# Compressed scores per block, uf written as x2 comes, token scale ahead of later splits, last stores on two queues

## The chip, the cores and the metric

The kernel runs on one core of one Trainium2 chip. The metric is the device time of one execution in microseconds; lower is better. The core's engines run their own instruction streams in order and wait for one another by semaphores: PE (TensorE) multiplies, DVE (VectorE) and ACT (ScalarE) work on elements, POOL (GpSimd) adds a few tiles, SP (SyncE) starts transfers.

## The reference

Two blocks follow one another on 256 tokens of width 2048. The first has one layer: attention with a compressed, a selected and a windowed branch (16 heads of 64, 4 key groups), a gating unit, a merge, and an added gate. The second puts 16 meta tokens in front (272 tokens) and has two layers, the first with a bidirectional state-space scan and a convolution of 31 taps, the second with neighbourhood attention. What the change touches:

```python
def first_block(x, p, ...):
    h = rms_norm(x, norm_g)                       # token scale
    q, kv, g_logits, z_a, uv, z_b, merge_logits = jnp.split(h @ w_in, SPLIT_IDX, axis=-1)
    ...
    kc = compress(k_c, pe_k, w1_k, w2_k)          # 15 blocks of keys
    sc = jnp.einsum('bqgrd,bngd->bgrqn', qb, kc) * scale   # compressed scores
    ...
    x = x + merged @ w_out
    x = x + jax.nn.sigmoid(x @ w_ple_gate) * (p @ w_ple)   # x2 in the kernel
    return rms_norm(x, final_g)

def second_block(x, meta_tokens, ...):
    h = jnp.concatenate([meta, x], axis=1)
    h = even_layer(h, ...)      # u = rmsnorm(h, norm_g); proj = u @ w_in; SSD scan, conv, w_out
    h = odd_layer(h, ...)       # neighbourhood attention
    return rmsnorm(h, final_norm_g)[:, N_META:]
```

## The kernel before

All activations lie with their features on the 128 partitions, 16 chunks of 128 features by 256 or 272 tokens. Most projections are "split": weights and activations are each written as a high and a low part (wh and wl, xh and xl, uh and ul), and `mm3` issues three matmuls for a chunk (L120 to L122). A weight piece of 512 KB is fetched by SP into one of four raw buffers; ACT writes its high half (L98), DVE its low half (L99). The first NFIRST = 2 projections of block 1 and the projections NAT = 0 to 3 of layer e take f32 operands and one f32 matmul for a chunk (L156); each shows as two records in the trace.

The order of the instructions on each engine is set by the scheduler of the framework from the order of the code and from priorities: `K.later(n)` puts a piece n places later in priority, `issue_after(ins)` keeps a piece behind an instruction. Each engine then runs its list strictly in order. Pools give out memory; a tile that takes the place of an earlier one waits for the earlier one's last reader.

**Start.** Squares of x are summed per token (`tok_sum`), the reciprocal root is made by `rsqrt` and `newton` on tiny tiles (rs_v, rs_y, ...), `r` is copied (L303), spread over the partitions by `diag` and the matmul `rb` (L218, L219), and copied by ACT to `rbs` (L305). Every projection of block 1 is multiplied by `rbs` as it leaves PSUM (`pj`, L319).

**Compressed scores.** The compressed keys are split into kcbd; the eight query projections are split into qh and ql; behind the last one a loop of 2 x 8 `mm3` of 32 columns makes `scps`, and DVE adds the bias (`sc`, L447).

**Boundary.** In the last stage of block 1, for each of 16 chunks, `w_pg`'s projection passes through ACT (`zt`), two DVE operations to x2 (L659, L660), its weighted square `sqw` (L663), and a plain square on ACT (`sq`). POOL adds the squares, weighted ones to s2 and plain ones to s1. Then PE makes the sum ss12 of s2 and the last sqw (L672, L673), and the token sums ss1 of s1 (L210, three matmuls of two records). Layer e reads ss12: `v` (L698), ten Newton steps on 272 columns, the scale r12 (a tile named tmp). `uf` is x2 times the two gains: the meta columns on DVE (L703), the chunks c % 4 == 1 on DVE (L707), the others on ACT (L709). `un` is uf times r12 (L714), split into uh (ACT, L163) and ul (DVE, L164). The projections 0 and 1 use uf, then `e_w_dt` uses uh and ul with 64 output rows (dt), then projections 2 and 3 use uf, then all others uh and ul. ss1 gives a second scale rbh, with which `norm_out` (L724) rewrites x2 as the residual and stores it to hres in four transfers.

**Later stages.** dt passes through a short chain (`steps`), its running sums go out to memory and come back, `dtp` transposes them; `cacc` is the short convolution, `cbps`, `xtp`, `yps` belong to the scan, with masks `m` from DVE.

**End.** The final scale is spread in `frb`, DVE multiplies h in five pieces (L1236), and SP stores each (L1237).

## Time and profile before

| | |
|---|---|
| time, median of 3 runs (lowest to highest) | 2270.6 us (2270.43 to 2271.83) |
| the profiled execution | 2271.78 us, its span 2269.9 us |
| PE busy | 2218.4 us, 98% of the span |
| DVE busy | 1639.2 us, 72% |
| ACT busy | 1162.1 us, 51% |
| POOL busy | 121.3 us, 5% |
| HBM read | 391.45 MB, 174 GB/s over the span |

The times in the views count from the span's start. Busy time of an engine says little by itself; what matters is what an engine waits for, and whether the engine that waits is the one on which the end depends. PEclk is the clock that PE was granted, as a share of full speed: 1.00 is 2.4 GHz, 0.50 is 1.2 GHz.

### The profile page before, as it was taken

How to read it: one execution, taken by the hardware profiler on the slowest of the kernel's cores; microseconds unless marked ns; L12 is line 12 of the kernel's file. 1: busy time of each engine (PE TensorE's matmuls, PEld its weight loads, DVE VectorE, ACT ScalarE, POOL GpSimd, SP SyncE). 2: the span in 40 equal slices, each digit the busy share in tenths (PEclk: the TensorE clock that was granted, in tenths of full speed). 3: DMA queues.
4: the chain of work that ended last, by engine and by line, in shares of the span. 5: the costliest groups of instructions: out<-in, count | busy, mean ns of one | idle time of the engine just before them, and what ended most of it. 6: DMA issues, size and time to landing. Idle time of an engine off the chain costs nothing.

```text
span 2269.9 us, 44011 instructions
## 1 busy us (share of the span) xinstructions
PE 2218.4 (98%) x17702; PEld 2156.0 (95%) x17702; DVE 1639.2 (72%) x2891; ACT 1162.1 (51%) x2039; POOL 121.3 (5%) x114
## 2 busy tenths in 40 slices
PE   8999999999999999999998998899999999999997
PEld 7998799999999998999998998899999999999997
DVE  6557777555555669999999888798776666666654
ACT  4446654444444444454557887645444545444453
POOL 0000000000000230000000010002011000000011
PEclk9999999999999999999999999999999999999999
DMA  7642455555556554564454556354655555545453
GB/s 279 217 148 94 138 190 184 187 184 187 186 195 209 186 171 148 199 220 174 174 177 151 175 176 181 123 177 151 202 176 189 172 172 173 171 166 171 160 172 121
DMA packets 126412, 398.71 MB, mean 176 GB/s; under 512 B 16832, under 2 KB 33664, under 8 KB 125696
## 3 DMA queue, kind: packets, MB, share of 16 engines
q1 hardware_dynamic: 126064, 395.89, 51.6%
q8 instruction: 139, 2.28, 0.4%
q14 instruction: 65, 0.53, 0.1%
q10 hardware_dynamic: 144, 0.01, 0.0%
HBM read 391.45 MB, written 4.40 MB: 174 GB/s over the span
## 4 chain that ended last, share of the span: by engine, by line
PE 93%; DVE 3%; ACT 2%; DMA 1%; issue 1%; POOL 0%; SPq 0%; DVEq 0%; ACTq 0%; POOLq 0%
PE acc L120 28%; PE acc L122 28%; PE acc L121 28%; PE acc L156 1%; DVE wl L99 1%; DMA rawf<-in_w_in_fm 1%; PE yps L959 1%; DVE vb L845 1%; ACT wh L98 1%; PE o_ps L1210 1%; PE pt_ps L506 0%; PE sp L120 0%; PE sp L122 0%; PE sp L121 0%; PE o_ps L1208 0%
## 5 line engine op out<-in xcount | busy, mean ns | idle before, releaser
L98 ACT ACTIVATE wh<-raw 128x1024 fp32r<-128x1024 f32 x674 | 713.1, 1059 | 955.1 <-PE acc L121 580.1
L99 DVE TENSOR_TENSOR wl<-raw,wh 128x1024 fp32r<-128x1024 f32 x674 | 828.1, 1230 | 404.4 <-ACT wh L98 399.4
L120 PE MATMUL acc<-uh,wh 128*128 128x272 f32 (+1 forms) x1488 | 436.3, 293 | 15.7 <-DVE za L995 8.2
L121 PE MATMUL acc<-ul,wh 128*128 128x272 f32 (+1 forms) x1488 | 434.3, 292 | 0.0
L122 PE MATMUL acc<-uh,wl 128*128 128x272 f32 (+1 forms) x1488 | 434.3, 292 | 0.0
L120 PE MATMUL acc<-xh,wh 128*128 128x256 f32 (+1 forms) x1136 | 322.3, 284 | 0.0
L121 PE MATMUL acc<-xl,wh 128*128 128x256 f32 (+1 forms) x1136 | 322.3, 284 | 0.0
L122 PE MATMUL acc<-xh,wl 128*128 128x256 f32 (+1 forms) x1136 | 321.1, 283 | 0.1
L120 PEld LDWEIGHTS acc<-uh,wh 128*128 128x128 f32 (+1 forms) x1488 | 280.8, 189 | 19.5 <-DVE za L995 8.9
L122 PE MATMUL acc<-ouh,wl 128*128 128x256 f32 (+1 forms) x1024 | 296.6, 290 | 0.0
L121 PE MATMUL acc<-oul,wh 128*128 128x256 f32 (+1 forms) x1024 | 294.6, 288 | 0.0
L120 PE MATMUL acc<-ouh,wh 128*128 128x256 f32 (+1 forms) x1024 | 293.8, 287 | 0.0
L121 PEld LDWEIGHTS acc<-ul,wh 128*128 128x128 f32 (+1 forms) x1488 | 280.6, 189 | 3.5 <-issue 2.3
L122 PEld LDWEIGHTS acc<-uh,wl 128*128 128x128 f32 (+1 forms) x1488 | 280.2, 188 | 3.2 <-issue 2.3
L120 PEld LDWEIGHTS acc<-xh,wh 128*128 128x128 f32 (+1 forms) x1136 | 213.8, 188 | 1.4 <-DVE pj L319 0.4
L122 PEld LDWEIGHTS acc<-xh,wl 128*128 128x128 f32 (+1 forms) x1136 | 214.4, 189 | 0.4 <-DVE wl L99 0.3
L121 PEld LDWEIGHTS acc<-xl,wh 128*128 128x128 f32 (+1 forms) x1136 | 213.6, 188 | 0.5 <-issue 0.2
L122 PEld LDWEIGHTS acc<-ouh,wl 128*128 128x128 f32 x1024 | 192.5, 188 | 2.6 <-issue 2.6
L120 PEld LDWEIGHTS acc<-ouh,wh 128*128 128x128 f32 x1024 | 192.9, 188 | 0.0
L121 PEld LDWEIGHTS acc<-oul,wh 128*128 128x128 f32 x1024 | 192.7, 188 | 0.0
L845 DVE SCALAR_TENSOR_TENSOR vb<-early,par,vb 128x257 f32<-128x257 f32 (+9 forms) x330 | 150.3, 500 | 1.1 <-ACT vb L829 0.7
L204 POOL TENSOR_TENSOR sq<-sq 128x272 f32<-128x272 f32 (+1 forms) x44 | 50.6, 1150 | 741.0 <-issue 450.3
(417 smaller groups left out, 4295.7 us busy)
## 6 DMA issues: line engine op xcount, KB each, us to landing
raw<-in_e_w_in SPq DMA_DIRECT2D x184, 512.0 KB, 3.6
raw<-in_w_in_fm SPq DMA_DIRECT2D x140, 512.0 KB, 3.6
raw<-in_o_w_in SPq DMA_DIRECT2D x128, 512.0 KB, 3.9
raw<-in_e_w_out SPq DMA_DIRECT2D x64, 512.0 KB, 4.5
raw<-in_w_up SPq DMA_DIRECT2D x32, 512.0 KB, 3.6
raw<-in_w_out SPq DMA_DIRECT2D x32, 512.0 KB, 4.4
raw<-in_w_pg SPq DMA_DIRECT2D x32, 512.0 KB, 4.2
raw<-in_o_w_out SPq DMA_DIRECT2D x32, 512.0 KB, 4.4
```

The lines of the kernel that those rows point to most:

```text
L98: nc.scalar.activation(wh, raw, AF.Copy)
L99: ins = nc.vector.tensor_tensor(wl, raw, wh.bitcast(F32), op=ALU.subtract)
L120: mm(out, lh, rh, start=start, stop=False)
L121: mm(out, lh, rl, start=False, stop=False)
L122: mm(out, ll, rh, start=False, stop=stop)
L156: self.nc.tensor.matmul(a, raws[c // 8][:, c % 8, :], x(c), start=c == 0, stop=c == 15)
L204: self.nc.gpsimd.tensor_tensor(acc, acc, sq, op=ALU.add)
L845: ins = nc.vector.scalar_tensor_tensor(v[:, lo:hi], u[:, lo + o : hi + o], par(K, "e_dw_w", 31 * b + k), v[:, lo:hi], op0=ALU.mult, op1=AL ...
L959: prev = nc.tensor.matmul(o, w, m, start=False, stop=k >= 6, skip_group_check=True).ins
L1210: nc.tensor.matmul(o_ps[64 * g : 64 * g + 64, ts], vt[:, 2 * t, 64 * g : 64 * g + 64], pt[:, g, :], start=False, stop=True, skip_group_che ...
```

## The change

Six edits, in the order of the code:

- A pool "f" holds one place that sqs, cmpA, kbd, ml, uf, bc, zb, bl and oh take one after another; before, they had places in the layers' own pools.
- The token scale: the projection i == 3 is issued behind the copy of r.
- Compressed scores: kcbd is one f32 tile, and behind each query projection two f32 matmuls on the unsplit q write its 2 x 32 columns of scps. The mm3 loop is gone.
- uf: written by ACT chunk by chunk as x2 comes, and its meta columns ahead of the loop. The sums ss12 stand in a `later(40)`.
- dt's transposes (`turned(0, dt)`) come right behind dt, those of cs stay where they were.
- The last stores: six pieces, in turn on SP's and ACT's queues. The scratch for transfers that engines describe themselves is set to 8192.

```diff
-LATER = [1000, 1500, 100]
+LATER = [1000, 1500, 100, 40]
...
+    def ftile(self, name, dt=F32, shape=(P, 16, T2)):
+
+        return self.fpool.tile(list(shape), dt, tag="f", name=name)
...
-        nc.vector.tensor_copy(r, K.rsqrt(ss[:, 0:2], 1.0 / D, EPS1))
+        r_ins = nc.vector.tensor_copy(r, K.rsqrt(ss[:, 0:2], 1.0 / D, EPS1)).ins
...
-                ps = K.proj(a["w_in_fm"][i], XH, XL, S)
+
+                with tc.issue_after(r_ins) if i == NFIRST + 1 else nullcontext():
+                    ps = K.proj(a["w_in_fm"][i], XH, XL, S)
...
-            K.split(kcbd[0][gs, :, g, 0:15], kcbd[1][gs, :, g, 0:15],
-                    cps[gs, :32].rearrange("q (p n) -> q p n", p=2)[:, :, 0:15])
+            nc.scalar.activation(kcbd[gs, :, g, 0:15], cps[gs, :32].rearrange("q (p n) -> q p n", p=2)[:, :, 0:15], AF.Copy)
...
+        scps = K.ps.tile([P, 2, S], F32, tag="t", bufs=2, name="scps")
         for j in range(8):
-            K.split(qh[:, j, :], ql[:, j, :], pj(0.125))
+            q = pj(0.125)
+            K.split(qh[:, j, :], ql[:, j, :], q)
+            for t in range(2):
+                nc.tensor.matmul(scps[:, t, 32 * j : 32 * j + 32].rearrange("q (g n) -> q g n", g=2),
+                                 q[:, 128 * t : 128 * t + 128], kcbd[:, j // 4], start=True, stop=True)
...
-        scps = K.ps.tile([P, 2, S], F32, tag="t", bufs=2, name="scps")
-        for t in range(2):
-            ts = slice(128 * t, 128 * t + 128)
-            for j in range(8):
-                p = j // 4
-                K.mm3(scps[:, t, 32 * j : 32 * j + 32].rearrange("q (g n) -> q g n", g=2), qh[:, j, ts], ql[:, j, ts],
-                      kcbd[0][:, p], kcbd[1][:, p], True, True)
...
+        uf = K.uf = K.ftile("uf")
+        nc.vector.tensor_tensor(uf[:, :, 0:META], x2[:, :, 0:META], par(K, "e_norm_g", 0, 16)[:, :, None].to_broadcast([P, 16, META]),
+                                op=ALU.mult)
         for m in range(16):
...
             nc.vector.tensor_tensor(x2[:, m, META:], t, pre, op=ALU.add)
+            nc.scalar.activation(uf[:, m, META:], x2[:, m, META:], AF.Copy, scale=feg[:, m : m + 1])
...
-        sums = K.ps.tile([P, 512], F32, tag="t", bufs=2, name="ss12")[:, :T2]
-        nc.tensor.matmul(sums, K.ones, s2, start=True, stop=False, skip_group_check=True)
-        nc.tensor.matmul(sums[:, META:], K.ones, sq, start=False, stop=True, skip_group_check=True)
-        K.feg, K.sums = feg, sums
+        with K.later(LATER[3]):
+            sums = K.ps.tile([P, 512], F32, tag="t", bufs=2, name="ss12")[:, :T2]
+            nc.tensor.matmul(sums, K.ones, s2, start=True, stop=False, skip_group_check=True)
+            nc.tensor.matmul(sums[:, META:], K.ones, sq, start=False, stop=True, skip_group_check=True)
+        K.sums = sums
         with K.later(LATER[0]):
...
-        uf = t16("e5", "uf")
+        uf = K.uf
...
-        for c in range(NCH):
-            if c % 4 == 1:
-                nc.vector.tensor_scalar(uf[:, c, META:], x2[:, c, META:], feg[:, c : c + 1], None, op0=ALU.mult)
-            else:
-                nc.scalar.activation(uf[:, c, META:], x2[:, c, META:], AF.Copy, scale=feg[:, c : c + 1])
...
             nc.vector.scalar_tensor_tensor(dt, pl, 2.0, zr, op0=ALU.mult, op1=ALU.add)
             yield 1.0
+            turned(0, dt)
+            yield 1.0
...
-        for lo, hi in ((0, 2), (2, 4), (4, 8), (8, 12), (12, 16)):
+        for k, (lo, hi) in enumerate(((0, 2), (2, 4), (4, 8), (8, 12), (12, 14), (14, 16))):
             v = h3[:, lo:hi, :]
             nc.vector.tensor_tensor(v, v, rb[:, None, :S].to_broadcast([P, hi - lo, S]), op=ALU.mult)
-            nc.sync.dma_start(out[:, lo:hi, :], v)
+            (nc.scalar if k % 2 else nc.sync).dma_start(out[:, lo:hi, :], v)
...
-    nc = bacc.Bacc("TRN2", target_bir_lowering=False, num_devices=1)
+    nc = bacc.Bacc("TRN2", target_bir_lowering=False, num_devices=1, dynamic_dma_scratch_size=8192)
```

The changed file has up to six lines more ahead of the same code, so its line numbers are higher by up to six (the split matmuls are L125 to L127, the f32 ones L161, the token sum L215).

PE at the boundary, before: behind the last w_pg matmul stand the two sums (ss with 272 and 256 columns), the three token sums, 32 f32 matmuls on uf, and then dt (acc of 64 rows).

```order
L122 MATMUL acc<-x1h,wl 128x256
L672 MATMUL ss_9979<-s_8621,ones 128x272
L673 MATMUL ss_9979<-sqw,ones 128x256
L210 MATMUL ss_9982<-ones,s_8620 128x1 x3
L156 MATMUL acc<-uf,rawf 128x272 x32
L120 MATMUL acc<-uh,wh 64x272
```

PE at the same place, now:

```order
L127 MATMUL acc<-x1h,wl 128x256
L679 MATMUL ss_9964<-s_8588,ones 128x272
L161 MATMUL acc<-uf,rawf 128x272 x13
L680 MATMUL ss_9964<-sqw,ones 128x256
L161 MATMUL acc<-uf,rawf 128x272 x19
L215 MATMUL ss_9967<-ones,s_8587 128x1 x3
L125 MATMUL acc<-uh,wh 64x272
```

The second sum and the token sums moved behind 13 and behind all 32 of the uf matmuls. The wait of v on DVE is for the third token sum in both programs.

PE at the end of dt, now (before, all 32 matmuls of projections 2 and 3 stand together behind dt's last one):

```order
L125 MATMUL acc<-uh,wh 64x272
L161 MATMUL acc<-uf,rawf 128x272 x10
L126 MATMUL acc<-ul,wh 64x272
L127 MATMUL acc<-uh,wl 64x272
L125 MATMUL acc<-uh,wh 64x272
L126 MATMUL acc<-ul,wh 64x272
L127 MATMUL acc<-uh,wl 64x272
L161 MATMUL acc<-uf,rawf 128x272 x22
```

Ten of them moved ahead of dt's last five matmuls, behind the first matmul of its chunk 14.

DVE between the un and ul of dt, now: the sixteen operations of norm_out (x with rbh) stand here, ahead of the ul of chunks 5, 6 and 7. Before, they stand some 175 rows later in DVE's list, behind the convolution's first part.

```order
L714 TENSOR_TENSOR un<-uf,tmp 128x272
L724 SCALAR_TENSOR_TENSOR x_8585<-x_8585,par,rbh 128x256 x5
L169 TENSOR_TENSOR ul<-un,uh 128x272
L714 TENSOR_TENSOR un<-uf,tmp 128x272
L724 SCALAR_TENSOR_TENSOR x_8585<-x_8585,par,rbh 128x256 x6
L169 TENSOR_TENSOR ul<-un,uh 128x272
L714 TENSOR_TENSOR un<-uf,tmp 128x272
L724 SCALAR_TENSOR_TENSOR x_8585<-x_8585,par,rbh 128x256 x5
L169 TENSOR_TENSOR ul<-un,uh 128x272
```

The first five moved ahead of eleven of the sixteen ul that dt's matmuls wait for, the last five ahead of nine.

## Rows read from the trace of the kernel before

**Rows 1.** The page, parts 1 and 4: busy time by engine, and the chain.

```profile
PE 2218.4 (98%) x17702; PEld 2156.0 (95%) x17702; DVE 1639.2 (72%) x2891; ACT 1162.1 (51%) x2039; POOL 121.3 (5%) x114
...
PE 93%; DVE 3%; ACT 2%; DMA 1%; issue 1%; POOL 0%; SPq 0%; DVEq 0%; ACTq 0%; POOLq 0%
```

**Rows 2.** Waits of PE: whom for, us in total, times, the longest.

```profile
PE acc L120 <- DVE za L995: 8.2, 2, 6.3
...
PE yps L959 <- DVE m L907: 5.0, 2, 3.2
PE acc L120 <- DVE cacc L876: 4.7, 3, 2.0
...
PE acc L120 <- DVE pj L319: 2.3, 1, 2.3
```

**Rows 3.** Windows by stage: length, busy us by engine, PEclk, DMA share, GB/s.

```profile
900.00:1180.00 280.00, 280.00 (x2249) 279.66 (x2248) 269.24 (x479) 133.18 (x181) 9.79 (x9) 1.00 0.54 189
1180.00:1230.00 50.00, 42.29 (x336) 40.22 (x335) 47.88 (x100) 35.65 (x88) 1.61 (x2) 1.00 0.47 155
```

**Rows 4.** Windows of the boundary: PE, PEld, DVE, ACT, POOL, PEclk, DMA, GB/s.

```profile
849.87:854.89 5.02, 2.15 (x13) 1.26 (x11) 2.21 (x6) 1.68 (x5) 0.72 (x1) 0.95 0.01 2
854.89:857.60 2.71, 2.71 (x6) 2.13 (x7) 2.71 (x14) 2.71 (x8) 0.00 (x0) 0.50 0.08 16
...
870.90:877.54 6.64, 6.64 (x55) 6.55 (x54) 5.82 (x16) 2.65 (x6) 0.00 (x0) 1.00 0.53 197
877.54:892.00 14.46, 14.46 (x66) 11.99 (x65) 13.60 (x29) 3.87 (x6) 0.00 (x0) 1.00 0.39 139
892.00:900.00 8.00, 8.00 (x65) 7.96 (x64) 7.44 (x13) 3.76 (x6) 0.00 (x0) 1.00 0.77 275
```

**Rows 5.** Waits of PE at the boundary, 849.8 to 892 us.

```profile
PE ss L673 <- DVE sqw L663: 1.5, 1, 1.5
PE acc L156 <- ACT uf L709: 1.0, 1, 1.0
```

**Rows 6.** Tiles v, un and ul: ns min/median/max, first and last start.

```profile
L698 DVE TENSOR_SCALAR v<-ss x1: 441/441/441, 854.0 to 854.0; 128x272 f32<-128x272 f32 x1
...
L714 DVE TENSOR_TENSOR un<-uf,tmp x16: 435/440/444, 860.0 to 872.4; 128x272 f32<-128x272 f32 x16
...
L164 DVE TENSOR_TENSOR ul<-un,uh x16: 435/439/444, 861.1 to 873.7; 128x272 fp32r<-128x272 f32 x16
```

**Rows 7.** Groups of 849.8 to 892.1: busy us, mean ns, idle before, releaser.

```profile
L709 ACT ACTIVATE uf<-x,feg 128x256 f32<-128x256 f32 x12 | 4.9, 500 | 1.8 <-PE ss L210 1.8
L707 DVE TENSOR_SCALAR uf<-x,feg 128x256 f32<-128x256 f32 x4 | 1.1, 349 | 0.0
L698 DVE TENSOR_SCALAR v<-ss 128x272 f32<-128x272 f32 x1 | 0.4, 441 | 2.1 <-PE ss L210 2.1
```

**Rows 8.** Groups of 972 to 981: the output operations.

```profile
L724 DVE SCALAR_TENSOR_TENSOR x<-x,par,rbh 128x256 f32<-128x256 f32 x16 | 6.6, 486 | 0.0
```

**Rows 9.** Windows at the start and at the compressed scores, columns as before.

```profile
38.40:42.00 3.60, 3.60 (x9) 2.82 (x10) 3.60 (x8) 0.12 (x1) 0.00 (x0) 0.53 0.81 267
...
144.30:147.70 3.40, 3.40 (x19) 3.40 (x19) 0.00 (x0) 0.00 (x0) 0.00 (x0) 0.52 0.44 154
147.70:150.50 2.80, 2.80 (x27) 2.80 (x26) 0.00 (x0) 0.00 (x0) 0.00 (x0) 0.97 0.00 0
```

**Rows 10.** The chain at the start: start us, length us, what.

```profile
35.69 1.07 ACT wh L98
...
36.78 0.62 DVE wl L99
...
37.93 0.43 DVE pj L319
```

**Rows 11.** Windows at the end, columns as before.

```profile
2263.00:2264.00 1.00, 0.00 (x0) 0.00 (x0) 1.00 (x1) 0.00 (x0) 0.00 (x0) 0.50 0.77 275
...
2265.00:2266.00 1.00, 0.00 (x0) 0.00 (x0) 0.24 (x1) 0.00 (x0) 0.00 (x0) 0.50 1.04 365
```

More of the change, by code (lines that the diff above doesn't have):

```diff
@@ L262, in block1 @@
         wk = ctx.enter_context(tc.tile_pool(name="b1w", bufs=2))
-        def t16(tag, dt=F32, nm=None):
-            return big.tile([P, 16, S], dt, tag=tag, name=nm or tag)
         def t8(tag, dt=F32, nm=None):
@@ L331, in block1 @@
         pe = {nm: const_in("pe" + nm, "pe_" + nm) for nm in ("k", "v")}
[L332 removed]
+        cmpA = K.ftile("cmpA", shape=(P, 2, 2, 16, 2, 16))
         nc.gpsimd.memset(cmpA[:, :, 1, :, :, 15], 0.0)
@@ L385, in block1 @@
         cbias = const_in("cbias", "c_cbias", tag="sb")
-        kcbd = [wk.tile([P, 2, 2, 16], F32R, tag="kcbd%d" % i, bufs=1, name="kcbd%d" % i) for i in range(2)]
-        for i in range(2):
-            nc.vector.memset(kcbd[i].bitcast(F32), 0.0)
+        kcbd = wk.tile([P, 2, 2, 16], F32, tag="kcbd", bufs=1, name="kcbd")
+        nc.vector.memset(kcbd, 0.0)
         hidbd = wk.tile([P, 2, 4, 2, 16], F32, tag="hidbd", bufs=1, name="hidbd")
@@ L424, in block1 @@
         nc.sync.dma_start(dmat, a["c_dist"])
-        kbd = big.tile([P, 2, 2, 2, 2, S], F32R, tag="b3", name="kbd")
+        kbd = K.ftile("kbd", F32R, (P, 2, 2, 2, 2, S))
         nc.gpsimd.memset(kbd.bitcast(F32), 0.0)
@@ L595, in block1 @@
                 zs.append(gate(g + 2))
-        mh, ml = K.hpool.tile([P, 16, S], F32R, tag="h", name="mh"), t16("b3", F32R, "ml")
+        mh, ml = K.hpool.tile([P, 16, S], F32R, tag="h", name="mh"), K.ftile("ml", F32R, (P, 16, S))
         for m in range(16):
@@ L773, in layer_e, with turned @@
         dt0 = wk.tile([P, 2, 16], F32, tag="dt0", bufs=1, name="dt0")
+        def turned(k, src):
+            tp = K.ps.tile([P, 512], F32, tag="t", bufs=2, name="dtp")
+            for i, (s0, s1) in enumerate(TT2[1:]):
+                nc.tensor.transpose(tp[:, 64 * i : 64 * i + 64], src[:, s0:s1], K.ident[:64, :64])
+            for q in range(4):
+                r0 = 32 * (q // 2) + q % 2
+                nc.tensor.matmul(tp[32 * q : 32 * q + 32, 128:144], src[:, 0:32], K.ident[:64, r0 : r0 + 31 : 2],
+                                 start=True, stop=True, skip_group_check=True)
+            nc.scalar.activation(dtT[:, k].rearrange("p i r -> p (i r)"), tp[:, 0:128], AF.Copy)
+            nc.scalar.activation(dt0[:, k], tp[:, 128:144], AF.Copy)
         def steps():
@@ L802, in steps @@
             nc.sync.dma_start(csd, cs)
-            for k, src in enumerate((dt, cs)):
-                tp = K.ps.tile([P, 512], F32, tag="t", bufs=2, name="dtp")
-                for i, (s0, s1) in enumerate(TT2[1:]):
-                    nc.tensor.transpose(tp[:, 64 * i : 64 * i + 64], src[:, s0:s1], K.ident[:64, :64])
-                for q in range(4):
-                    r0 = 32 * (q // 2) + q % 2
-                    nc.tensor.matmul(tp[32 * q : 32 * q + 32, 128:144], src[:, 0:32], K.ident[:64, r0 : r0 + 31 : 2],
-                                     start=True, stop=True, skip_group_check=True)
-                nc.scalar.activation(dtT[:, k].rearrange("p i r -> p (i r)"), tp[:, 0:128], AF.Copy)
-                nc.scalar.activation(dt0[:, k], tp[:, 128:144], AF.Copy)
+            turned(1, cs)
             yield 1.0
@@ L883, in conv5 @@
             return nc.vector.scalar_tensor_tensor(dst, t, 1.0, acc, op0=ALU.add, op1=ALU.mult)
-        bc = big.tile([P, 2, 8, T2], F32, tag="e5", name="bc")
+        bc = K.ftile("bc", shape=(P, 2, 8, T2))
         for k in range(2):
@@ L1125, in layer_o @@
         QH, QL = (lambda c: qv(uh, c)), (lambda c: qv(ul, c))
-        oh = big.tile([P, 16, S], F32R, tag="o2", name="oh")
+        oh = K.ftile("oh", F32R, (P, 16, S))
         ol = big.tile([P, 16, S], F32R, tag="o3", name="ol")
```

14 lines of the change are left out of this document (6 added, 8 removed).

## The prediction

> **What bounds the kernel now.** I read the page first: TensorE (PE) is busy for 98% of the span and 93% of the chain that ended last runs through it [rows 1]. So the time is PE's own work plus the few places where PE stands still or runs at its lower clock, and an edit counts only if it takes matmul time away, closes such a place, or opens one. The waits of PE name the places [rows 2]: the reader is to see a handful of them, none over 8.2 us in all. The table by stage shows where they lie [rows 3]: from 900 to 1180 us PE never stops, while DVE is busy for 269.24 of 280 us, so there DVE has little slack and PE none. From 1180 to 1230 PE is busy for only 42.29 of 50 us. The stage that the change rebuilds most is the boundary between block 1 and the next layer, and I split that into pieces [rows 4] and looked for what releases its first instructions [rows 5 to 7].
>
> The profiled execution took 2271.78 us (span 2269.9 and 1.9 around it); the median of the three runs is 2270.6. I build the sum on the profiled run and take off 1.2 us at the end. A measurement can tell about 0.2%, 4.5 us, from no change.
>
> **The boundary: the largest term, and a loss.** Before, the last gate projection is followed by the two sums, the three token sums, 32 f32 matmuls on uf, dt, and 32 more on uf. From 849.87 to 854.89 PE is busy for only 2.15 us, waiting 1.5 for sqw and 1.0 for uf; the clock is then 0.50 for 2.71 us [rows 4, 5]. The change takes both waits away: uf is written as x2 comes, so uf matmuls can run while sqw is made. The copies on ACT, 0.5 us each [rows 7] and now sixteen, run beside the projections of an engine that is busy for 51% of the span [rows 1], and I cost them at nothing; if that cover were gone, each would hold a weight split for 0.5 us. Taken alone this would give 2.5 us of waiting and half of 2.71, about 3.9.
>
> But the order now puts the three token sums behind all 32 uf matmuls, and the first Newton step v is released by the token sums, not by the sums that it reads: v starts at 854.0 [rows 6], and what ended the 2.1 us of idle time before it was line L210, the token sum [rows 7]. In the changed program v's wait stands at the same point, the third token sum. Queued behind v on DVE are the whole Newton chain and all un and ul; PE waits for these in dt. I work it through:
> - PE's own work up to the token sums: 2.15 us as before, plus 32 uf matmuls. From 877.54 to 892.00 such 32 take 14.46 us [rows 4], 0.452 each. Token sums end at 849.87 + 2.15 + 14.46 = 866.5, and v starts there instead of at 854.0.
> - From v to the first un took 6.0 us (854.0 to 860.0 [rows 6]), of which 1.5 were DVE's share of uf, now gone (four copies of 1.1 in all [rows 7], and the meta columns, costed like one un at 0.4): un at 871.0. Then un and the ACT half of the split, about 0.44 each: first dt matmul at 871.9. PE has nothing else in its queue, so it stands still for 5.4 us.
> - The 16 pairs un, ul took 14.1 us (860.0 to 874.1 [rows 6]), with a weight split of 1.2 in them that now lies before: 12.9. The 16 output operations of line L724, 6.6 us at 973 to 980 before [rows 8], now stand ahead of the sixth, seventh and eighth ul. So the last ul ends at 871.0 + 12.9 + 6.6 = 890.5. dt before needed 6.64 us of PE [rows 4]; now it goes at DVE's pace.
> - Ten uf matmuls of the second set stand behind chunk 14's first matmul, whose uh is there at about 889.2: they end at 893.7. The rest of dt, five matmuls of 0.123 (65 records in 8.00 us from 892 to 900 [rows 4]), ends at 894.3, and 22 uf matmuls at 0.452 end at 904.3, where it was 892.00.
>
> That is **+12.3 us**. Ends: +10.5 if the DVE pairs go faster than I take them by about 2 us, +14.5 if the clock is at its lower level (1.2 instead of 2.4 GHz) through the ten uf matmuls, as it was for 2.71 us behind the idle stretch at 849.87 to 854.89 [rows 4]. The four stores that go with L724 move ahead of the next weight loads in SP's queue; they leave at about 885, 19 us before the weights behind them are wanted at 904, so I cost them at nothing; if that were not enough, each us late is a us lost. DVE gets the 6.6 us back in 973 to 980, where PE was not waiting for it.
>
> The Trainium skill (TensorE: Matmul & The Clock Gate, section "HAM oscillation — how this bites in real kernels") holds that idle gaps of PE bring its clock down, which speaks against this change: the order makes a new gap. Here the row agrees (0.50 behind the gap before); by the rule the gap of 5.4 us takes the upper end, 14.5, and by the row's own length of 2.71 us, spent mostly in a dt that waits for DVE anyhow, next to nothing is added.
>
> **Compressed scores.** Before, 48 matmuls of 32 columns run in one piece of work; 27 records take 2.80 us [rows 9], 0.104 each, so 5.0 us in all. In and behind them the clock reads about half twice, 0.52 for 3.40 us from 144.30 and the same again some 7 us later [rows 9]; each costs half of that, 1.7. After, 16 f32 matmuls of the same width stand in twos between projections. Their price is not in the trace. An f32 matmul is two records, so at least 2 x 0.104 = 0.21; 272 columns take 0.452 in f32 and 0.123 split [rows 4], so at most 3.7 x 0.104 = 0.38. I take 0.25, nearer to the lower end, because a record of 32 columns is nearly as long as one of 272 (0.104 to 0.123) and so hardly goes by its columns: 4.0 us, 1.0 less than before. They stand far apart, so I take both clock drops as gone: **-4.4 us**. Ends: -5.1, and +1.0 where the drops stay and the price is the upper one. The tile scps is now held over eight projections; the DVE addition that reads it still follows the last one.
>
> **Token scale at the start.** DVE now does the chain to r in one piece, ahead of the weight splits of the projection i == 3; ACT's rbs leaves one weight half earlier. Before, pj starts at 37.93, behind an ACT weight half of 1.07 us and a DVE split [rows 10]; PE waits 2.3 us for it [rows 2], and then runs 3.60 us at 0.53 [rows 9]. With one ACT weight half less the wait goes to about 1.2. The lower clock costs 1.7; half of that I count. **-2.0 us**. Ends: -2.9 (the clock stays up), and +0.6, if the split that is moved behind r, some 1.7 us later, releases its raw buffer later and the load that takes its place then arrives late.
>
> **The last stores.** From 2264 to past 2268 the DMA engines are full at about 365 GB/s; one row of the four stands [rows 11]. Only the dip ahead of that (a share of 0.77 from 2263 to 2264) and the start can be filled, some 0.4 us: **-0.4 us**, ends -1.3 (the last piece is half as large, and lands that much sooner) and +0.1. The Trainium skill (DMA: Bandwidth & Descriptors, section "Issuing engines are not separate DMA queues") says that transfers from several engines run on the same 16 DMA engines and that only issue time is saved. The full rows agree; by it the term is 0 to -0.4, without it a second queue might have been worth up to 1.3.
>
> **The rest.** dt's transposes come earlier, and xtp, cbps and yps shift by 10 to 37 matmuls against the rest from 1195 to 1405; behind that PE's order is the same. Before, yps waits 5.0 us for m and the projections 4.7 for cacc [rows 2]. I take 0, with ends -5 and +6. The one f place that uf, bc, zb and oh share replaces places that were shared already, but for oh, whose predecessor is read out long before.
>
> Sum: -2.0 - 4.4 + 12.3 - 0.4 + 0 = +5.5; 2271.8 + 5.5 = 2277.3, and with the 1.2 off **2276.1**.
>
> **The rivals.**
> A. v is not held: it starts once the sums it reads are there, at about 857. Then un starts at 861.5, the last ul ends at 881.0, ten uf matmuls run from 879.7 to 884.2, and the rest of dt and 22 uf end at 894.8: +2.8 instead of +12.3, total 2266.6, just faster or the same. For it: v reads only the sums. Against: the release [rows 7] and the place of v's wait. If L724 also stayed out of the way, PE would be the bound: 849.87 + 2.15 + 14.46 + 6.64 + 14.46 = 887.6, -4.4, total 2259.4. The order rules that out.
> B. The lead of DVE pays later. PE arrives at 900 some 12 us later; DVE some 16.4 later with 6.6 of its work done, so DVE gains about 2.5 us on PE. If that lasts to 1200, the 7.7 us that PE lacks there [rows 3] shrink by 2.5, and with yps placed better by up to 5 more: 2268.6 to 2273.6. It decides where DVE is not held back by the weight buffers that PE frees.
> C. yps comes before its m is ready. Groups placed 1.2 to 4.6 us earlier meet the same DVE, and PE, which waits 5.0 us there now, waits up to 6 us more: 2282.
> D. Small f32 matmuls do not spare the clock: the scores term is +1.0, total 2281.5.
>
> **How the numbers follow.** Forecast case, 2271 to 2281 on its own: 0.50. A: 0.22, of which 0.06 for its second half; it is the likeliest rival, since the whole loss hangs on one wait. B: 0.12. C: 0.09. D: 0.07. Slower by over 0.2% means over 2275.1: of the forecast case 0.30, and C and D: 0.46. Faster means under 2266.1: of A 0.14, of B 0.01, of the forecast case, with its other terms at their lower ends, 0.03: 0.18. Within: 0.36. The range leaves out A's second half and the far ends of C and D: 2263 to 2283.
>
> **What would show it.** Right: v after the token sums at about 866.5, PE idle for 5 us there, dt from 872 to 894, split projections from 904; no clock drop at 141 to 155; PE's wait for pj near 1.2. Wrong: v before 860, un and ul done by 881, or PE busy through 866 to 890; then A holds. If the boundary costs 12 us and the total doesn't show it, the stage from 1180 on gave it back (B).

## The result and the profile after

The changed kernel took **2283.9 us** (median of five executions, 2279.87 to 2285.07), the kernel before 2270.6: a ratio of 1.0055, 95% interval 1.0043 to 1.0067. It is slower by over 0.2%, as forecast, by 13.3 us where 5.5 were forecast, and 0.9 us above the range. It was timed three more times beside the experiments; all 19 executions have a median of 2281.4, the 115 of the kernel before that ran beside it and the experiments 2271.3. These 10 us are what has to be explained.

The profiled execution took 2279.87 us, its span is 2277.8: 7.9 us more than the span of before. The lines of the page that answer to [rows 1], engines and then chain, read:

```profile
PE 2221.1 (98%) x17686; PEld 2153.9 (95%) x17686; DVE 1640.1 (72%) x2885; ACT 1162.8 (51%) x2043; POOL 113.4 (5%) x114
PE 93%; DVE 3%; ACT 2%; DMA 1%; issue 0%; SPq 0%; POOL 0%; DVEq 0%; ACTq 0%; POOLq 0%
```

Nothing in them tells of the change; the shares are those of before. The waits of PE do (engine, tile and line that waited, what it waited for, us in all, times, longest), to be held against [rows 2]:

```profile
PE acc L125 <- DVE za L1000: 8.2, 2, 6.3
...
PE acc L125 <- ACT uh L168: 5.5, 1, 5.5
PE acc L126 <- DVE ul L169: 5.4, 3, 2.5
...
PE acc L125 <- DVE cacc L881: 3.0, 2, 2.0
PE yps L964 <- DVE m L912: 3.0, 2, 2.5
PE acc L127 <- DVE wl L104: 2.7, 1, 2.7
...
PE acc L125 <- DVE pj L323: 1.7, 1, 1.7
```

Two waits are new: 5.5 us for the first uh and 5.4 for three of the ul, both in dt. Those for m and cacc are smaller than before, by 3.7 in all. The tiles at the boundary (durations in ns as lowest, median and highest, then first and last start) show why dt waits:

```profile
L705 DVE TENSOR_SCALAR v<-ss x1: 442/442/442, 859.5 to 859.5; 128x272 f32<-128x272 f32 x1
L714 DVE TENSOR_TENSOR un<-uf,tmp x16: 435/442/447, 864.0 to 881.2; 128x272 f32<-128x272 f32 x16
L169 DVE TENSOR_TENSOR ul<-un,uh x16: 437/443/445, 865.1 to 882.2; 128x272 fp32r<-128x272 f32 x16
L724 DVE SCALAR_TENSOR_TENSOR x<-x,par,rbh x16: 484/485/486, 868.9 to 876.2; 128x256 f32<-128x256 f32 x16
L161 PE MATMUL acc<-uf,rawf x128: 391/392/497, 843.6 to 897.2; 128*128 128x272 f32 x128
```

DVE's waits from 840 to 920 us name the cause, a v that stands behind the token sum:

```profile
DVE v L705 <- PE ss L215: 5.5, 1, 5.5
```

The same moments of the two profiled executions, in us after the span's start, give the account:

| moment | before | after | difference | since the row above |
|---|---|---|---|---|
| first hps matmul (start done) | 73.6 | 71.3 | -2.3 | -2.3 |
| last zt (front done) | 850.1 | 843.4 | -6.7 | -4.4 |
| last uf matmul (boundary done) | 892.0 | 897.2 | +5.2 | +11.9 |
| last u of the gates | 1065.1 | 1073.0 | +7.9 | +2.7 |
| last yb (scan done) | 1462.4 | 1471.1 | +8.7 | +0.8 |
| first multiply of the stores | 2260.6 | 2268.5 | +7.9 | -0.8 |
| end of the span | 2269.9 | 2277.8 | +7.9 | 0.0 |

So the sum came true up to the end of the boundary (+5.2, where the terms for start, scores and boundary give +5.9), and 2 to 3 us more were lost behind it. What is then still lacking of the 10 to 13 us lies between executions of one and the same program. A span times one minus its mean granted clock is the most that the lower clock can have cost; where PE stands still anyway, as during the last stores [rows 11], it costs nothing. What is left of the span I call the time at full clock. Their means, and the times at equal clock (executions in brackets):

| | clock | lost to it, at most | at full clock | at 0.987, 0.988 | at 0.989 | at 0.990 | at 0.991 | at 0.992 to 0.994 |
|---|---|---|---|---|---|---|---|---|
| before, 115 | 0.9902 | 22.2 us | 2247.1 us | none | 2273.7 (40) | 2270.7 (36) | 2270.5 (26) | 2266.3 (13) |
| after, 19 | 0.9893 | 24.4 us | 2254.9 us | 2284.4 (5) | 2282.6 (5) | 2278.5 (5) | 2279.1 (4) | none |

At equal clock the change costs 8 to 9 us, about what the profile shows; the rest is that its executions get less clock. Its four profiled executions, 2278.6 to 2279.9, all ran at 0.990 or 0.991, so no trace of this kernel shows where the others lose theirs. The trace of f1_dt_back below, with the same order up to 880 us and a clock of 0.989, shows one such place.

### The profile page after: what moved, and what is told of

Its sections match the earlier page's. It is cut to its first block, busy times and chain, and to the rows that moved or that the text cites. A ratio compares the mean times of both kernels' runs of the same rounds, so it can differ in the third digit from the quotient of the medians.

```text
span 2277.8 us, 43969 instructions
## 1 busy us (share of the span) xinstructions
PE 2221.1 (98%) x17686; PEld 2153.9 (95%) x17686; DVE 1640.1 (72%) x2885; ACT 1162.8 (51%) x2043; POOL 113.4 (5%) x114
## 4 chain that ended last, share of the span: by engine, by line
PE 93%; DVE 3%; ACT 2%; DMA 1%; issue 0%; SPq 0%; POOL 0%; DVEq 0%; ACTq 0%; POOLq 0%
PE acc L125 28%; PE acc L127 28%; PE acc L126 28%; PE acc L161 1%; PE yps L964 1%; DMA rawf<-in_w_in_fm 1%; DVE wl L104 1%; PE o_ps L513 1%; PE pt_ps L507 1%; PE o_ps L1215 1%; PE sp L125 0%; PE sp L127 0%; PE sp L126 0%; ACT wh L103 0%; PE o_ps L1213 0%
## 5 line engine op out<-in xcount | busy, mean ns | idle before, releaser
L125 PE MATMUL acc<-uh,wh 128*128 128x272 f32 (+1 forms) x1488 | 438.7, 295 | 20.2 <-DVE za L1000 8.2
L127 PE MATMUL acc<-uh,wl 128*128 128x272 f32 (+1 forms) x1488 | 435.9, 293 | 0.0
L125 PE MATMUL acc<-xh,wh 128*128 128x256 f32 (+1 forms) x1136 | 321.9, 283 | 0.0
L127 PE MATMUL acc<-xh,wl 128*128 128x256 f32 (+1 forms) x1136 | 319.7, 281 | 0.0
L125 PEld LDWEIGHTS acc<-uh,wh 128*128 128x128 f32 (+1 forms) x1488 | 282.7, 190 | 24.8 <-DVE za L1000 8.9
L127 PE MATMUL acc<-ouh,wl 128*128 128x256 f32 (+1 forms) x1024 | 296.6, 290 | 0.0
L125 PE MATMUL acc<-ouh,wh 128*128 128x256 f32 (+1 forms) x1024 | 293.7, 287 | 0.0
L127 PEld LDWEIGHTS acc<-uh,wl 128*128 128x128 f32 (+1 forms) x1488 | 282.2, 190 | 2.6 <-issue 1.5
L125 PEld LDWEIGHTS acc<-xh,wh 128*128 128x128 f32 (+1 forms) x1136 | 212.4, 187 | 1.5 <-issue 0.5
L127 PEld LDWEIGHTS acc<-xh,wl 128*128 128x128 f32 (+1 forms) x1136 | 213.0, 188 | 0.5 <-issue 0.2
L127 PEld LDWEIGHTS acc<-ouh,wl 128*128 128x128 f32 x1024 | 192.5, 188 | 2.6 <-issue 2.6
L125 PEld LDWEIGHTS acc<-ouh,wh 128*128 128x128 f32 x1024 | 192.9, 188 | 0.0
```

What stands on the lines that cost most here:

```text
L125: mm(out, lh, rh, start=start, stop=False)
L127: mm(out, ll, rh, start=False, stop=stop)
```

## The experiments

All are given as the ratio to the kernel before, run beside them, with its 95% interval. "Lost to clock" is the mean over a kernel's executions, again the most that it can have cost. "Scan" and "end" come from its profile: how much longer than in the first profile of before the stretch from the last uf matmul to the last yb is (570.4 us there), and the one from that yb to the span's end (807.5 us).

| kernel | median us | ratio | lost to clock | scan | end |
|---|---|---|---|---|---|
| after, 19 executions | 2281.4 | 1.0055, 1.0052, 1.0032, 1.0049 | 24.4 | +3.5 | -0.8 |
| e12_before_r2 (before, again) | 2272.2 | 1.0001 | 22.4 | +1.6 | 0.0 |
| e2_no_boundary | 2271.8 | 0.9996 | 21.5 | +4.9 | -3.8 |
| e6_scores_only | 2269.5 | 0.9992 | 19.5 | +1.3 | 0.0 |
| e7_start_scores | 2270.7 | 0.9995 | 20.4 | +6.4 | +0.1 |
| e3_tok_first | 2276.3 | 1.0022 | 21.8 | +6.8 | +0.7 |
| e5_norm_late | 2276.5 | 1.0024 | 19.2 | +2.4 | +1.9 |
| e4_tok_norm | 2269.3 | 0.9992 | 16.4 | +1.8 | +1.6 |
| e8_best | 2272.3 | 1.0006 | 21.7 | +11.4 | -1.5 |
| e9_filled | 2279.5 | 1.0034 | 18.6 | +2.0 | +1.7 |
| f1_dt_back | 2280.6 | 1.0048 | 26.4 | +1.7 | -0.7 |
| f2_six_norm | 2266.1 | 0.9974 | 16.0 | +5.6 | -3.8 |
| f3_six_norm_l1200 | 2266.4 | 0.9984 | 17.6 | +8.4 | -3.8 |

**The changed kernel again** (no edit), three times, and the kernel before once more:

> The changed kernel once more, for a second profile and the spread of its time. Theory (order at the boundary): the boundary, from the first sum to the first split projection behind the f32 ones, takes 54.4 us again, as in the first profile of the changed kernel, against 42.1 before; 1.005 to 1.006 of the time before. Rival (the clock): the boundary is about the same length, but the granted clock is at half in other places than in the first profile (there 863 to 871, 874 to 881 and 1034 to 1038), and the span moves by up to 5 us with it.

> The changed kernel once more, for a third profile. Theory (clock): a slower execution shows the lower clock for longer, between 860 and 900 or in the scan's stage, at the same waits. Rival (a wait that comes and goes, as the one of 2.7 us at 1543): the same clock, another list of waits.

> The changed kernel once more, for a fourth profile, with the same two theories: the lower clock for longer at the same waits, or the same clock and another list of waits.

> The kernel before once more, for a second profile. Theory (clock and a wait that comes and goes set the spread of single executions): same order, same places, the lower clock longer or shorter by 2 to 4 us. Rival: the spread lies in the transfers, and the start or the weight waits differ.

Ratios 1.0052 (1.0035 to 1.0068), 1.0032 (1.0018 to 1.0046), 1.0049 (1.003 to 1.0068), and 1.0001 (0.9989 to 1.0014) for before. The table of moments repeats: the last uf matmul comes 5.7, 4.8 and 3.9 us later than before, the end 6.9, 7.7 and 6.8. The second profile of before is 3.4 us longer than its first, as its theory had it; 1.8 of that are there by the end of the boundary, where the clock over the window is 0.92 against 0.96 in the first profile, and 1.6 arise in the scan stage. So the account above is good to about 2 us a stage. No profiled repeat of the changed kernel took longer than 2279.6 us, so the two theories on its longer executions stay undecided.

**Everything but the boundary.** The kernel before with the edits at the start, in the scores, in dt's transposes and at the last stores; uf and the sums stay as they were.

```diff
 # before, with: token scale ahead of split i == 3, f32 scores per block,
 # turned(0, dt) behind dt, six stores on two queues, scratch 8192
 # without: pool "f", uf written as x2 comes, sums in later(40)
```

> All edits but the boundary one: uf is made in layer e as before, in the layer's own pool, and the sums and token sums stand ahead of the uf matmuls as before. Theory (the whole loss is the boundary's order): start and scores together gain 6.7 us as in the first profile of the changed kernel, and nothing else loses, so 2263 to 2265, ratio 0.997. Rival (the later stage loses by itself, through the moved transposes and the order behind them): 2268 or more, ratio 0.999 to 1.002.

Ratio 0.9996 (0.9985 to 1.0007), median 2271.8. So the boundary's edits (with the pool "f") hold the whole loss: with them 1.0032 to 1.0055, without them no change. But the theory's 2263 to 2265 missed, and the time is the rival's: what start and scores gain is not there at the end. In the profile the front gains 7.4 us, the boundary costs nothing, the scan takes 4.9 back. The executions lie in two groups, five at 2265.8 to 2267.2 and seven at 2271.7 to 2273.2; the profiled one is of the first. The profile of f2_six_norm below shows a place that may be a part of it.

**The scores alone, and the scores with the token scale.**

```diff
-            K.split(qh[:, j, :], ql[:, j, :], pj(0.125))
+            q = pj(0.125)
+            K.split(qh[:, j, :], ql[:, j, :], q)
+            for t in range(2):
+                nc.tensor.matmul(scps[...], q[:, 128 * t : 128 * t + 128], kcbd[:, j // 4], start=True, stop=True)
```

> The kernel before with the scores edit alone. Its order behind the boundary is close to that of before (output operations at the same place of DVE's list, dt's transposes 30 rows earlier). Theory A (the scores gain 4.4 to 5 and it lasts where the later order is kept): ratio 0.998, 2266 to 2267. Theory B (whatever is gained ahead of the boundary is given back in the scan's stage, because DVE sets its pace): ratio 0.9995 to 1.0005.

> The kernel before with the scores edit and the token scale edit. Together, not one by one, they move dt's transposes by 300 rows and the output operations ahead by some 140 rows. Theory A (this move of the later order eats the gain): 7 us earlier at the boundary, 2 to 3 us at the end of the scan's stage, ratio 0.9990 to 1.0000, worse than the scores alone. Theory B: 7 us earlier at the boundary; ratio about equal to that of the scores alone.

Ratios 0.9992 (0.9981 to 1.0002) and 0.9995 (0.9983 to 1.0008). The front is 5.1 us shorter in the one profile and 5.2 in the other; alone, the scores keep 4.1 of it to the end, and with the token scale added the scan takes 6.4 back. In that second execution the token scale adds nothing to the front: PE waits 2.3 us for pj and runs at 0.57 from 38 to 42 us, as before. No gain clear of the noise is left of either part. For the scores alone the interval leaves out theory A's 0.998 by a hair and takes in B's range, while the profile, which keeps 4.1 of 5.1 us, speaks for A; the two kernels can't be told apart by their times. So neither theory is settled.

**The token sums ahead.** The changed kernel with the token sums two matmuls of uf behind the sum that v reads, not behind all 32.

```diff
-        with K.later(LATER[0]):
+        with K.later(LATER[3]):
             ss = K.ps.tile([P, 512], F32, tag="o", bufs=1, name="ss1")
```

> The changed kernel with one edit: the three token sums stand two uf matmuls behind the second sum, not behind all 32; the 16 output operations stay among the ul. Theory (v is held by the token sums): v starts some 8 us earlier relative to the first sum, PE does not stand still for 5.5 us ahead of dt, and the boundary shrinks from 54.4 to about 46; 0.3% to 0.5% faster than the changed kernel. Rival (DVE's own pace in dt, with the output operations in it, sets the end, or v waits for something else): v moves, or not, but the boundary stays above 52.

Ratio 1.0022 (1.001 to 1.0034). The tiles of DVE, as above:

```profile
L705 DVE TENSOR_SCALAR v<-ss x1: 431/431/431, 853.2 to 853.2; 128x272 f32<-128x272 f32 x1
L714 DVE TENSOR_TENSOR un<-uf,tmp x16: 429/431/442, 857.7 to 874.8; 128x272 f32<-128x272 f32 x16
L169 DVE TENSOR_TENSOR ul<-un,uh x16: 428/431/433, 858.8 to 875.9; 128x272 fp32r<-128x272 f32 x16
```

v comes 6.3 us sooner than in the changed kernel, every un and ul 6.3 with it, and the boundary ends 6.4 sooner; PE no longer waits for uh. The mean time falls by 5.5 us, 0.24%, where 0.3% to 0.5% were expected. The wait of v on the token sums is shown to cost that much.

**norm_out out of DVE's chain.** The changed kernel with the 16 output operations behind the last ul.

```diff
             for m in range(16):
-                nc.vector.scalar_tensor_tensor(x2[:, m, META:], ...)
+                with tc.issue_after(order[NCH - 1]):
+                    nc.vector.scalar_tensor_tensor(x2[:, m, META:], ...)
```

> The changed kernel, its token sums behind all 32 uf matmuls as they are, but the 16 output operations wait for the last ul. Theory (two costs add up: v held, and 6.6 us of output operations in DVE's chain): the boundary is 54.4 less 6.6, about 48, PE still stands still for 5.5 us ahead of dt; ratio about 1.002. Rival (the output operations were hidden in waits that the held v makes anyway): boundary above 52, ratio 1.004 or more.

> As the run before, and the 16 output operations wait for the last ul. Theory: nothing of DVE's chain is then later than PE's own work; the boundary is 2.15 + 14.46 + 6.64 + 14.46, about 38, shorter than before the change; 2257 to 2261, ratio 0.995. Rival (the output operations were hidden, or moving them holds up the next weight splits): no better than the run before.

Ratio 1.0024 (1.0014 to 1.0034). Here v keeps its place behind the token sums, and ul runs through without a stop:

```profile
L705 DVE TENSOR_SCALAR v<-ss x1: 440/440/440, 861.2 to 861.2; 128x272 f32<-128x272 f32 x1
L169 DVE TENSOR_TENSOR ul<-un,uh x16: 429/439/445, 866.9 to 877.7; 128x272 fp32r<-128x272 f32 x16
```

From v to the last ul it is 16.5 us, where the changed kernel needs 22.7: 6.2 less, against the 6.6 of the prediction's term. The mean falls by 5.0. With both edits (e4_tok_norm) the mean falls by 12.0, to 2269.2, ratio 0.9992 (0.9982 to 1.0001): the two costs add up, to a little more than 5.5 and 5.0, and the whole loss is gone. The pool "f" and the uf written early stay in this kernel, so it was the order that cost the time. From the last zt to the last uf matmul it takes 41.1 us, where before takes 41.9 and the changed kernel 53.8. Faster than before, as its theory had it (2257 to 2261), it is not: 41.1 is more than the 38 expected, and of the shorter front the scan and the end take 3.4 back.

**The idle place filled.** The changed kernel with 11 f32 matmuls of 272 columns, whose results nobody reads, ahead of dt, and one ahead of each chunk up to 13.

```diff
+                for _ in range(11 if c == 0 else 1 if c < 14 else 0):
+                    with self.tc.issue_after(ins) if ins else nullcontext():
+                        ins = fill()
             ins = self.mm3(back(a), *w(c), back(xh(c)), back(xl(c)), c == 0, c == k - 1)
```

> The changed kernel with matmuls that do nothing useful (their results are not read): 11 f32 ones of 272 columns ahead of dt's first, and one behind each of dt's chunks up to 13, so that PE is busy where it stood still for 5.5 us and ran in small pieces. Ten of the later uf matmuls fall behind dt for it, some 4 us. Theory (the clock): the granted clock stays up through dt and the uf matmuls behind it, the split projections begin at 896 to 898 as in the profile of the changed kernel, and the median of the time falls to 2275 to 2279, because the executions without a profile of the changed kernel lose 4 us to the clock here. Rival (the clock here is no part of it): the boundary is as long or 4 us longer, and the median stays at 2281 to 2286.

Ratio 1.0034 (1.0022 to 1.0046), median 2279.5. The window over the boundary (busy us of PE, its weight loads, DVE, ACT and POOL, then the granted clock, the DMA share and GB/s), first of the changed kernel, then of this one:

```profile
843.00:897.00 54.00, 42.84 (x194) 34.94 (x194) 38.66 (x102) 14.43 (x30) 0.73 (x1) 0.87 0.35 128
```

```profile
843.00:897.00 54.00, 49.51 (x233) 40.40 (x232) 39.35 (x107) 13.86 (x29) 0.72 (x1) 0.94 0.33 116
```

PE is busy for 6.7 us more and the clock goes from 0.87 to 0.94; over the whole kernel 18.6 us at most are lost to it and not 24.4. But the last uf matmul comes at 898.8, 1.6 us later, since the filling itself holds back what follows dt; the time at full clock is 2259.6, 4.7 more. The median lies in neither range. The mean falls by 1.1 us, and the interval overlaps those of the changed kernel, so no gain is shown; what a kept clock alone would be worth here stays open, because the filling costs time too.

**The mended boundary, first try.** Sums and token sums early, the other uf matmuls from the seventh on held back behind them, norm_out put far behind, among the convolution's blocks.

```diff
-        with K.later(LATER[3]):
+        with K.later(0):
             sums = ...
-        with K.later(LATER[0]):
+        with K.later(0):
             ...
-                return K.proj_f32(a["e_w_in"][i], lambda c: uf[:, c, :], T2), True
+                return K.proj_f32(a["e_w_in"][i], lambda c: uf[:, c, :], T2, None, K.tok_ins if i < 2 else None, 0 if i else 6), True
-        K.run(norm_out(), LATER[0])
+            if b == 6:
+                K.run(norm_out(), 0)
```

> The changed kernel with the sums and the token sums behind six uf matmuls, and the output operations behind the convolution's seventh block. Theory (order at the boundary): v at about 848, PE without a wait of over 1 us until dt's tail, split projections from 881 to 884, against 892 before and 897 in the changed kernel; ratio 0.994 to 0.997. Rival (given back in the scan's stage): split projections from 884 all the same, but ratio 0.998 to 1.000.

Ratio 1.0006 (0.9997 to 1.0016): my theory missed. The boundary ends 9.6 us sooner than before, and the scan takes 11.4 back. PE's waits from the first yps to the last yb, to be held against [rows 2] with 5.0 for m and 4.7 for cacc, say where:

```profile
PE yps L968 <- DVE m L916: 9.7, 3, 4.8
PE acc L125 <- DVE za L1004: 7.5, 1, 7.5
PE acc L125 <- DVE cacc L885: 5.1, 2, 4.3
PE acc L125 <- ACT zb L1052: 4.4, 1, 4.4
```

In all they are 5 us longer than the same waits in the profile of before (26.7 against 21.7). PE comes sooner to masks for which DVE isn't ready; the rest of the 11.4 is not accounted for. norm_out isn't what keeps DVE there: it runs at 982 to 988, near its old place [rows 8].

**dt's transposes back.** The changed kernel with one priority changed, so that dt's transposes lie about where they were (996 us and not 1030).

```diff
-LATER = [1000, 1500, 100, 40]
+LATER = [1000, 1100, 100, 40]
```

> The changed kernel with dt's transposes put less far back (1100 in place of 1500), so that they stand where they stood before, some 290 rows earlier; 18 rows of PE's list differ behind the boundary, no more. Theory (the late place of the transposes, in pieces between projections, costs what is lost behind the boundary): 1 to 3 us faster than the changed kernel, ratio 1.003 to 1.004. Rival (the order of xtp and yps, which stays): within 1 us of the changed kernel, ratio 1.004 to 1.0055.

Ratio 1.0048 (1.0031 to 1.0064), median 2280.6 of five executions; a sixth, of 4258 us, is left out. The rival held, no gain is shown. In the profile of the changed kernel the transposes end at 1034, and the window behind them, this one, is the only one between 900 and 1180 with a lower clock:

```profile
1033.00:1038.00 5.00, 5.00 (x28) 4.83 (x27) 4.43 (x11) 4.36 (x14) 0.00 (x0) 0.66 0.43 140
```

That is 1.7 us of the 2.7 lost between 897 and 1073. In f1_dt_back no such window follows, and 0.9 are lost there. But the three repeats of the changed kernel, with the transposes where they were, lose only 1.2 there, at a clock of 1.00. The drop belongs to one execution and not to the place.

This profile shows another such drop. Up to 880 us the order of f1_dt_back is that of the changed kernel, but its front ends 2.0 us later (845.4 and not 843.4), all of it lost at the start, where PE waits 2.3 us for pj and the lower clock is back:

```profile
38.00:42.00 4.00, 4.00 (x12) 3.09 (x12) 4.00 (x9) 0.68 (x1) 0.00 (x0) 0.57 0.64 203
```

**The mended boundary, second try.** As e8_best, but norm_out directly behind the last ul (the edit of e5_norm_late), so that the order behind the boundary stays near to that of before. The second kernel has 1200 for the 1500 in LATER as well.

```diff
 # sums, token sums and uf matmuls as in e8_best; norm_out as in e5_norm_late
-LATER = [1000, 1500, 100, 40]
+LATER = [1000, 1200, 100, 40]     # f3_six_norm_l1200 only
```

> The changed kernel with the sums and token sums behind six uf matmuls, and the output operations behind the last ul; its order in the scan's stage is nearer to that of before (93 rows differ) than in the mended kernels up to now. Theory (the scan's order eats the gain): split projections at 882 to 884, 8 to 10 us early, and most of it kept, 4 to 8 us early at the end, ratio 0.9965 to 0.998. Rival (an early arrival is given back whatever the order): 8 to 10 us early at the boundary, 0 to 2 at the end, ratio 0.999 to 1.0005.

> As the run before, with 1200 in place of 1500 for dt's steps: the transposes stand some 210 rows earlier, and 60 rows differ from the order of before. Theory (the scan's order): as good as the run before or better by 1 to 2 us, ratio 0.996 to 0.998. Rival (an early arrival is given back): ratio 0.999 to 1.0005, as the run before.

Ratios **0.9974** (0.9965 to 0.9984) and 0.9984 (0.997 to 0.9997): 2266.1 and 2266.4 us. Both beat the kernel before; the second misses its range, and the two are not clearly apart. The boundary of f2_six_norm:

```profile
L707 DVE TENSOR_SCALAR v<-ss x1: 442/442/442, 850.0 to 850.0; 128x272 f32<-128x272 f32 x1
L716 DVE TENSOR_TENSOR un<-uf,tmp x16: 433/436/439, 857.0 to 867.8; 128x272 f32<-128x272 f32 x16
L162 PE MATMUL acc<-uf,rawf x128: 392/392/497, 846.0 to 883.9; 128*128 128x272 f32 x128
```

and its window there, which stands against 0.87 and 42.84 busy of 54 in the changed kernel:

```profile
843.00:897.00 54.00, 53.77 (x319) 47.63 (x318) 45.05 (x113) 20.78 (x37) 0.73 (x1) 1.00 0.54 184
```

PE never waits and keeps its full clock; the boundary ends 8.1 us sooner than before. The time is what the theory gave, but its reason is not borne out: the scan stage takes 5.6 of the 8.1 back here too (8.4 in f3), and the end then comes 3.8 sooner for a cause that no edit aimed at. The window behind the scan, of before and then of f2_six_norm:

```profile
1500.00:1560.00 60.00, 55.91 (x422) 55.20 (x421) 50.61 (x88) 29.66 (x55) 16.04 (x16) 0.94 0.56 178
```

```profile
1500.00:1560.00 60.00, 58.68 (x457) 58.40 (x456) 50.38 (x92) 32.05 (x56) 17.97 (x16) 0.97 0.61 195
```

Before, PE waits 2.7 us for a weight's low half (wl), and the granted clock over the 60 us is 0.94 where it is 0.97 in f2_six_norm: up to 1.8 more. In the profiles of f2, f3 and e2 this wait is absent: DVE starts its first wl 4.2 us sooner than before (1539.07, before 1543.24), while the stage itself, taken at the last zb, comes only 2.5 sooner. The 1.7 between them lie in one row of DVE ahead of that wl, six subtractions for the low part of yb (start us, length us, what), of before and then of f2_six_norm:

```profile
1535.75 5.48 DVE L164 TENSOR_TENSOR al<-yb,ah 128x272 fp32r<-128x272 f32 x6
```

```profile
1533.32 3.73 DVE L170 TENSOR_TENSOR al<-yb,ah 128x272 fp32r<-128x272 f32 x6
```

Before, POOL adds squares without a pause from 1533.7 to 1540.9, nearly all through these six; in f2_six_norm it pauses twice between 1534.8 and 1536.9. That its adds slow DVE here was not tested. In the profiles of all other kernels the wait is there, as in the changed one (2.7 in its waits above). The two groups of e2_no_boundary lie 5.9 us apart, somewhat more than this place, and its slower group has no trace. f2_six_norm loses 16.0 us at most to the clock against 22.2, and its time at full clock, 2248.0, is not below the 2247.1 of before. By this account its gain is a kept clock and one wait that falls away, not less work.

## Why the prediction was wrong where it was

**The boundary, +12.3: right, 11.9.** By the prediction's own steps, with the front's 6.7 us taken off: v at 859.8 (measured 859.5), the first un at 864.3 (864.0), the end of the last ul at 883.8 (882.6), the end of the last uf matmul at 897.6 (897.6). PE's idle stretch was put at 5.4 and is 5.5, and its releaser is as named: v waits 5.5 us for the token sum on DVE, though it reads only the sums. Rival A, a v that isn't held, is refuted in the changed kernel and shown to be what the edits of e3 and e5 bring about. The two causes that the steps named, the hold of v and norm_out's 6.6 us, were each undone alone and gave 5.5 and 5.0 us of mean time, both together 12.0.

The clock at this place is 0.87 over 54 us, 7 us lost, yet the term is no larger than without such a loss. The Trainium skill (TensorE: Matmul & The Clock Gate, section "HAM oscillation — how this bites in real kernels") says that gaps bring the clock down. The trace agrees, but the upper end of 14.5 that was reckoned from it did not come: the low clock fell on a dt that waited for DVE, and the ten uf matmuls on which that end rested ran at the full clock again (this window):

```profile
882.00:886.50 4.50, 4.47 (x20) 3.72 (x21) 3.64 (x9) 1.11 (x3) 0.00 (x0) 1.00 0.00 0
```

**The start, -2.0: right, -2.3, but not in every execution.** PE's wait for pj went from 2.3 to 1.7, not to 1.2, and the clock drop behind it is gone altogether (this window, and [rows 9] with 0.53):

```profile
38.00:42.00 4.00, 4.00 (x19) 3.25 (x18) 4.00 (x8) 0.26 (x1) 0.00 (x0) 1.00 0.66 229
140.00:160.00 20.00, 20.00 (x166) 19.74 (x165) 17.26 (x36) 11.05 (x26) 0.00 (x0) 1.00 0.44 155
```

The repeats of the changed kernel give -2.1 to -3.5; the profiles of the other kernels with this edit give -2.9 to +0.1, and in four of them (e5, e7, f1 and f2, -0.7 at best) the drop is there again.

**The scores, -4.4: right, -4.4.** Both drops near 144 and 151 are gone (the second line). Rival D is refuted. The records of the small matmuls are longer than I took them, though:

```profile
L442 PE MATMUL scps<-kcbd,pj x32: 191/275/276, 101.5 to 144.7; 128*128 128x32 f32 x32
```

I took 0.25 us for two records, and one alone reads 0.19 to 0.28. The term came out whole, so most of a record lies beside its neighbours; what a small matmul costs there isn't to be read from its record.

**The stores, -0.4: nothing, 0.0.** From the first multiply to the end it is 9.3 us before and after. The Trainium skill (DMA: Bandwidth & Descriptors, section "Issuing engines are not separate DMA queues") says that transfers run on the same 16 DMA engines whichever engine starts them, and that a second one saves only the time of starting them. Here the trace agrees: the 9.3 us did not change.

**The rest, 0: the first step that failed, and the smaller one.** I took nothing, with ends of -5 and +6, for all that lies behind the boundary, because PE's order there is nearly the same. The profile shows +2.7 between 897 and 1073 and +0.8 up to the last yb, then -0.8. It is within the ends, but not in the forecast. Of the 2.7, 1.7 are the clock drop of one execution; in the three repeats it is 1.2. Rival B went the wrong way: the waits for m and cacc did shrink, by 3.7 (in the repeats by 2.3 to 3.6), and yet the stage became longer. Rival C's 2282 lies near the measured time, but its mechanism isn't there: the longer wait for m fell from 5.0 to 3.0 in all four profiles. Every kernel that was profiled lost something in the scan stage against the first profile of before, 1.3 to 11.4 us, before itself 1.6: its first profile was a good one there. Those that arrive sooner tend to lose more (e8 and f3 most, e6 and e4 little), so no rule is shown for it. Which rows of the order cost it stays open; putting dt's transposes back (f1) gave no gain.

**The base: the second step that failed, and the larger one.** Of the 7.8 us between 2276.1 and 2283.9, 2.6 lie in the profiled execution (8.1 longer than that of before, where 5.5 were forecast). The other 5.2 are in no term: I put the sum onto one profiled execution and took off 1.2 us, but the median of the first five lies 4.0 above their profiled one. The step assumes that both programs get the clock of the profiled execution in the others too. Before does in its first profile (2271.8 against a median of 2271.3), less so in its second (2275.1). After took 2278.6 to 2279.9 in its four profiled executions and up to 2286.2 in others. Its profiles are 5.6 us longer than the mean of before's two; all executions together are 10 us longer, the five of the first comparison 13. That these 5.6 so nearly meet the sum's 5.5 is in part luck: over all six profiles start and scores give 0.9 more than forecast, the boundary costs 1.0 less, and what follows it costs 1.6 where 0.4 less was forecast. Why the other executions get less clock stays open. One place is seen, the start, where f1_dt_back lost 2.0 us. The candidates besides are the places where PE waits or runs thin, which the change made more of; e9_filled, e5_norm_late and e4_tok_norm, which have fewer of them, lose 16.4 to 19.2 us at most to the clock, where the changed kernel loses up to 24.4.

**The range.** It held the median of all 19 executions but not that of the first five. Its upper end, 2283, took in the ends of the terms, but nothing for the spread of the executions, 2277.7 to 2286.2 in the changed kernel.

## What to carry to other kernels

A wait is set by its place in the queue: if an engine's first instruction of a chain stands behind another product of the same engine, moving that product moves the chain, whatever the chain reads. So when an order is rebuilt, follow the first instruction of the slower engine's chain and ask which of the faster engine's products it now stands behind, and what else was put between its links. And a gain ahead of a stage that two engines share is not yet a gain of the kernel: here fronts shorter by 5 to 7 us gave no gain clear of the noise in four kernels (e2, e4, e6 and e7), and in their profiles the scan took 1.3 to 6.4 us back. Last, time more than one execution of either kernel before a sum is put onto it.

## What was not expected of the hardware

- The executions of one program differ by their granted clock: before ran at 0.989 to 0.994, with means of 2273.7 us (40 executions) at the one end and 2262.9 (two) at the other. That is more than any kernel here gained on the kernel before.
- One wait of 2.7 us at 1543 us comes and goes: it is absent where DVE comes 1.7 us sooner against PE (4.2 less 2.5), and that time lies in six subtractions of equal shape, which take 3.73 us there and 5.48 before.
- The clock fell behind dt's transposes (0.66 from 1033 to 1038) while PE was busy throughout. In the three other profiles of the same program it stayed at 1.00 there (1025 to 1045).
